# Binary cross-entropy on one core: a small side block in 12-row transfers, and a last store of 128 rows

## The chip, the core and the metric

The kernel runs on one core of one Trainium2 chip. The metric is the device time of one execution in microseconds (us). The time before is 1864.81 us, the median of three runs (1864.67 to 1865.51).

## The reference

```python
def setup_inputs():
    return {
        "pred": np.random.uniform(0.01, 0.99, (8192, 8192)).astype(np.float32),
        "target": np.random.randint(0, 2, (8192, 8192)).astype(np.float32),
    }

def reference(pred, target):
    eps = 1e-7
    pred = np.clip(pred, eps, 1 - eps)
    return -(target * np.log(pred) + (1 - target) * np.log(1 - pred))
```

Two float32 matrices of 256 MiB each are read and one is written. Every target is 0 or 1, so the kernel computes -ln|p + t - 1|: for t = 1 that is -ln p, for t = 0 it is -ln(1 - p).

## The kernel before

The matrices are taken as flat runs of elements and cut into 40 chunks in flat order. A chunk of w columns is a tile of 128 partitions by w columns, and each partition's w elements are one contiguous run in memory. `plan` gives the widths: chunks 0 and 1 have 5120 columns (FIRST), chunks 2 to 36 have 14336 (BIG), chunks 37 and 38, named a and b, have 5632 (LAST), and chunk 39, named c, has 1024 (TAIL).

In on-chip memory pred lies in a ring of three BIG slots, `ring_p`, float32, and is turned into the output in place. Target lies in `ring_t`, one BIG slot of bf16. Both have 1024 columns more, behind the slots, for chunk c alone. Chunks a and b lie side by side in the slot that follows that of chunk 36.

For each chunk there are six kinds of steps:

- `load_t` (line 72): a transfer issued by GpSimd, which casts target from float32 to bf16 on its way.
- `load_p` (line 69): issued by GpSimd, and by SyncE for chunk 0 alone.
- `clip` (line 85): one VectorE pass, max and min.
- `log`: on VectorE p = (t - 1) + p (line 91), then Abs and Ln on ScalarE (lines 94 and 95).
- `back` (line 99): VectorE multiplies by -1.
- `store` (line 76): issued by GpSimd, and by SyncE for the last three chunks. Chunk c has `store_rows` (line 81) instead: three SyncE transfers, of 108, 12 and 8 partitions.

The order is written out by hand, inside `manual_schedule`: each engine takes its instructions in the order of the program, and waits only for the data that they need. A BIG chunk goes through `clip` and `log` in two halves (`(h, 2)`). Then the next chunk's target is loaded (it needs `ring_t` free, so it waits for line 91 on both halves), the two halves get `back`, the chunk is stored, and pred of the chunk after next is loaded into the slot that its predecessor in the ring has left. At the end, in iteration 36, target of a and b, pred of c and target of c are loaded in this order; pred of a and b is loaded one iteration earlier. Behind the loop the halves of a and b and the whole of c are interleaved by hand, and the stores of a, b and c go out on SyncE.

DMA transfers are carried out by 16 DMA engines. The profile lists GpSimd's transfers as the queue "software_dynamic" (q0) and SyncE's as "hardware_dynamic" (q1).

Of the kernel before, what the change touches and what calls it, by code (L numbers as in the profile page):

```python
# [1 line left out]

# [4 lines left out]

EPS = 1e-7

BIG = 14 * 1024  # L10
FIRST = 5 * 1024
LAST = 5632
TAIL = 1024
SLOTS = 3


def plan(total):
    n = (total - 2 * FIRST - 2 * LAST - TAIL) // BIG
    assert n > 4 and total == 2 * FIRST + n * BIG + 2 * LAST + TAIL
    spots = [(FIRST, 0, 0), (FIRST, FIRST, FIRST)]  # L20
    spots += [(BIG, k % SLOTS * BIG, 0) for k in range(1, n + 1)]
    end = (n + 1) % SLOTS * BIG
    spots += [(LAST, end, 0), (LAST, end + LAST, LAST)]
    return spots + [(TAIL, SLOTS * BIG, BIG)]


@with_exitstack
def kernel(
    ctx: ExitStack,
    tc: tile.TileContext,  # L30
    pred: bass.AP,
    target: bass.AP,
    out: bass.AP,
):
    nc = tc.nc
    fp32 = mybir.dt.float32
    bf16 = mybir.dt.bfloat16
    Alu = mybir.AluOpType
    Act = mybir.ActivationFunctionType
    P = nc.NUM_PARTITIONS  # L40

    R, C = pred.shape
    spots = plan(R * C // P)
    n = len(spots)
    widths = [s[0] for s in spots]
    cols = [sum(widths[:k]) for k in range(n)]

    def chunk(ap, k):
        flat = ap.rearrange("r c -> (r c)")
        return flat[cols[k] * P : (cols[k] + widths[k]) * P].rearrange("(p w) -> p w", p=P)  # L50

    pool = ctx.enter_context(tc.tile_pool(name="rings", bufs=1))
    ring_p = pool.tile([P, SLOTS * BIG + TAIL], fp32, name="ring_p", tag="ring_p")
    ring_t = pool.tile([P, BIG + TAIL], bf16, name="ring_t", tag="ring_t")
    warm = pool.tile([1, 8], fp32, name="warm", tag="warm")

    def spot(k, part=(0, 1)):
        w, c, _ = spots[k]
        i, m = part
        return ring_p[:, c + i * w // m : c + (i + 1) * w // m]  # L60

    def spot_t(k, part=(0, 1)):
        w, _, c = spots[k]
        i, m = part
        return ring_t[:, c + i * w // m : c + (i + 1) * w // m]

    def load_p(k):
        queue = nc.sync if k == 0 else nc.gpsimd
        queue.dma_start(out=spot(k), in_=chunk(pred, k))  # L69

    def load_t(k):
        nc.gpsimd.dma_start(out=spot_t(k), in_=chunk(target, k))  # L72

    def store(k):
        queue = nc.sync if k >= n - 3 else nc.gpsimd
        queue.dma_start(out=chunk(out, k), in_=spot(k))  # L76

    def store_rows(k):
        src, dst = spot(k), chunk(out, k)
        for first, last in ((0, 108), (108, 120), (120, 128)):  # L80
            nc.sync.dma_start(out=dst[first:last], in_=src[first:last])

    def clip(k, *part):
        p = spot(k, *part)
        nc.vector.tensor_scalar(  # L85
            out=p, in0=p, scalar1=EPS, scalar2=1 - EPS, op0=Alu.max, op1=Alu.min
        )

    def log(k, *part):
        p = spot(k, *part)  # L90
        nc.vector.scalar_tensor_tensor(  # L91
            out=p, in0=spot_t(k, *part), scalar=1.0, in1=p, op0=Alu.subtract, op1=Alu.add
        )
        nc.scalar.activation(out=p, in_=p, func=Act.Abs)  # L94
        nc.scalar.activation(out=p, in_=p, func=Act.Ln)  # L95

    def back(k, *part):
        p = spot(k, *part)
        nc.vector.tensor_scalar(out=p, in0=p, scalar1=-1.0, scalar2=None, op0=Alu.mult)  # L99

    with tc.manual_schedule():
        nc.vector.memset(warm, 1.0)  # L102
        load_t(0)
        load_p(0)
        load_t(1)
        load_p(1)
        load_p(2)
        nc.scalar.activation(out=warm, in_=warm, func=Act.Ln)  # L108
        for k in (0, 1):
            clip(k)  # L110
            log(k)
        load_t(2)
        back(0)
        store(0)
        back(1)
        store(1)
        load_p(3)
        a, b, c = range(n - 3, n)
        for k in range(2, n - 3):
            for h in (0, 1):  # L120
                clip(k, (h, 2))
                log(k, (h, 2))
            if k < n - 4:
                load_t(k + 1)
            else:
                load_t(a)
                load_t(b)
                load_p(c)
                load_t(c)
                back(k, (0, 2))  # L130
                for j in (a, b):
                    clip(j)
            if k < n - 4:
                back(k, (0, 2))
            back(k, (1, 2))
            store(k)
            if k + 2 < n - 3:
                load_p(k + 2)
            elif k + 2 == n - 3:
                load_p(a)  # L140
                load_p(b)
        log(a, (0, 2))
        log(a, (1, 2))
        clip(c)
        log(b, (0, 2))
        back(a, (0, 2))
        log(b, (1, 2))
        back(a, (1, 2))
        store(a)
        log(c)  # L150
        back(b, (0, 2))
        back(b, (1, 2))
        store(b)
        back(c)
        store_rows(c)


# [1 line left out]
_INS = ['pred', 'target']  # L159
_OUTS = [((8192, 8192), 'float32')]  # L160


# [23 lines left out]
```

## Time and profile before

| | |
|---|---|
| median of three runs | 1864.81 us (1864.67 to 1865.51) |
| the profiled execution's own time | 1864.33 us |
| its span, first to last instruction | 1862.6 us |
| VectorE (DVE) busy | 1121.6 us, 60% |
| ScalarE (ACT) busy | 902.4 us, 48% |
| GpSimd (POOL) busy | 178.5 us, 10% |
| bytes read from and written to HBM | 536.87 and 268.44 MB, 432 GB/s over the span |
| DMA packets | 17302, of which 592 in SyncE's queue |
| a BIG pred load, issue to landing | 44.3 us |
| a BIG target load, issue to landing | 31.3 us |
| a BIG store, issue to landing | 31.1 us |

Times are counted from the start of the span. An engine's busy time doesn't count waiting or the issuing of DMAs by a sequencer (SPq is SyncE's). The DMA row of the slices gives the mean busy share of the 16 DMA engines in tenths, where 9 is 90% or more. The GB/s in it counts what arrives, so a target load counts half of what it reads. The profile's rows carry no number of the DMA engine, but the trace has the start, length and size of each packet and the time of each semaphore update: a transfer over all 128 partitions posts 16 of these, one for each DMA engine's share.

### The profile page before, as it was taken

How to read it: one execution, taken by the hardware profiler on the slowest of the kernel's cores; microseconds unless marked ns; L12 is line 12 of the kernel's file. 1: busy time of each engine (PE TensorE's matmuls, PEld its weight loads, DVE VectorE, ACT ScalarE, POOL GpSimd, SP SyncE). 2: the span in 40 equal slices, each digit the busy share in tenths (PEclk: the TensorE clock that was granted, in tenths of full speed). 3: DMA queues.
4: the chain of work that ended last, by engine and by line, in shares of the span. 5: the costliest groups of instructions: out<-in, count | busy, mean ns of one | idle time of the engine just before them, and what ended most of it. 6: DMA issues, size and time to landing. Idle time of an engine off the chain costs nothing.

```text
span 1862.6 us, 707 instructions
## 1 busy us (share of the span) xinstructions
DVE 1121.6 (60%) x230; ACT 902.4 (48%) x156; POOL 178.5 (10%) x120
## 2 busy tenths in 40 slices
DVE  4666555555666566555555666566655555666565
ACT  4454444455555544444455555544444445555545
POOL 1111101111110011101111110011101111110020
DMA  9999999999999999999999999999999999999999
GB/s 346 347 371 355 356 352 355 356 355 354 359 375 374 375 372 355 355 355 355 355 355 355 357 374 374 374 372 355 355 356 355 357 357 356 357 373 376 375 352 356
DMA packets 17302, 671.15 MB, mean 360 GB/s; under 512 B 1936, under 2 KB 1936, under 8 KB 2320
## 3 DMA queue, kind: packets, MB, share of 16 engines
q0 software_dynamic: 16704, 662.18, 99.1%
q1 hardware_dynamic: 592, 8.91, 1.1%
q14 instruction: 6, 0.05, 0.0%
HBM read 536.87 MB, written 268.44 MB: 432 GB/s over the span
## 4 chain that ended last, share of the span: by engine, by line
DMA 60%; issue 35%; ACT 3%; DVE 2%; POOL 0%; POOLq 0%; DVEq 0%; PEldq 0%
DMA ring_t<-in_target_dram 57%; DMA ring_p<-in_pred_dram 4%; ACT ring_p L95 1%; ACT ring_p L94 1%; DVE ring_p L91 1%; DVE ring_p L99 0%; DVE ring_p L85 0%; POOL out_dram L76 0%; POOL ring_t L72 0%; POOLq L72 0%; POOL ring_p L69 0%; POOLq L76 0%; DVEq L91 0%; PEldq L181 0%
## 5 line engine op out<-in xcount | busy, mean ns | idle before, releaser
L94 ACT ACTIVATE ring_p<-ring_p 128x7168 f32<-128x7168 f32 (+3 forms) x77 | 452.0, 5870 | 942.1 <-DVE ring_p L91 942.1
L91 DVE SCALAR_TENSOR_TENSOR ring_p<-ring_t,ring_p 128x7168 f32<-128x7168 bf16 (+3 forms) x77 | 558.2, 7251 | 372.5 <-DMA ring_t<-in_target_dram 371.3
L99 DVE TENSOR_SCALAR ring_p<-ring_p 128x7168 f32<-128x7168 f32 (+3 forms) x77 | 285.4, 3706 | 329.4 <-ACT ring_p L95 329.4
L95 ACT ACTIVATE ring_p<-ring_p 128x7168 f32<-128x7168 f32 (+3 forms) x77 | 452.5, 5877 | 2.4
L85 DVE TENSOR_SCALAR ring_p<-ring_p 128x7168 f32<-128x7168 f32 (+3 forms) x75 | 284.6, 3794 | 24.0 <-DMA ring_p<-in_pred_dram 24.0
L76 POOL DMA_DIRECT2D out_dram<-ring_p x37 | 128.0, 3459 | 584.4 <-DVE ring_p L99 584.3
L72 POOL DMA_DIRECT2D ring_t<-in_target_dram x40 | 28.9, 722 | 1057.5 <-DVE ring_p L91 1056.7
L69 POOL DMA_DIRECT2D ring_p<-in_pred_dram x39 | 21.7, 558 | 2.5 <-issue 2.5
L108 ACT ACT_TABLE_LOAD x1 | 1.3, 1283 | 0.7 <-PEq L170 0.7
L102 DVE MEMSET warm<- 1x8 f32 x1 | 0.1, 65 | 0.8 <-PEq L170 0.8
L108 ACT ACTIVATE warm<-warm 1x8 f32<-1x8 f32 x1 | 0.2, 208 | 0.0
L170 POOL MEMSET const-float32-0.0<- 128x1 f32 x1 | 0.1, 99 | 0.2 <-issue 0.2
L170 POOL MEMSET const-bfloat16-1.0<- 128x1 bf16 x1 | 0.1, 102 | 0.0
L170 POOL MEMSET const-float32-1.0<- 128x1 f32 x1 | 0.1, 99 | 0.0
L170 POOL MEMSET const-uint8-127<- 128x1 uint8 x1 | 0.1, 99 | 0.0
## 6 DMA issues: line engine op xcount, KB each, us to landing
ring_p<-in_pred_dram POOLq DMA_DIRECT2D x35, 7168.0 KB, 44.3
out_dram<-ring_p POOLq DMA_DIRECT2D x35, 7168.0 KB, 31.1
ring_t<-in_target_dram POOLq DMA_DIRECT2D x35, 3584.0 KB, 31.3
ring_p<-in_pred_dram POOLq DMA_DIRECT2D x2, 2816.0 KB, 37.2
out_dram<-ring_p SPq DMA_DIRECT2D x2, 2816.0 KB, 14.7
out_dram<-ring_p POOLq DMA_DIRECT2D x2, 2560.0 KB, 28.7
ring_t<-in_target_dram POOLq DMA_DIRECT2D x2, 1408.0 KB, 26.5
ring_p<-in_pred_dram SPq DMA_DIRECT2D x1, 2560.0 KB, 13.1
```

The lines of the kernel that those rows point to most:

```text
L69: queue.dma_start(out=spot(k), in_=chunk(pred, k))
L72: nc.gpsimd.dma_start(out=spot_t(k), in_=chunk(target, k))
L76: queue.dma_start(out=chunk(out, k), in_=spot(k))
L85: nc.vector.tensor_scalar(out=p, in0=p, scalar1=EPS, scalar2=1 - EPS, op0=Alu.max, op1=Alu.min)
L91: nc.vector.scalar_tensor_tensor(out=p, in0=spot_t(k, *part), scalar=1.0, in1=p, op0=Alu.subtract, op1=Alu.add)
L94: nc.scalar.activation(out=p, in_=p, func=Act.Abs)
L95: nc.scalar.activation(out=p, in_=p, func=Act.Ln)
L99: nc.vector.tensor_scalar(out=p, in0=p, scalar1=-1.0, scalar2=None, op0=Alu.mult)
L102: nc.vector.memset(warm, 1.0)
L108: nc.scalar.activation(out=warm, in_=warm, func=Act.Ln)
L170: nc = _bacc.Bacc("TRN2", target_bir_lowering=False, num_devices=1)
```

## The change

A block of 24 rows by 896 columns, the last 21504 elements of the matrices, is taken out of chunk c, which becomes 856 columns wide (1024 - 24 x 896 / 128). It has two tiles of its own, `side_p` and `side_t`, both float32 and 128 by 896, of which only 24 partitions carry data: partitions 0, 9, ..., 99 the first 12 rows, partitions 1, 10, ..., 100 the other 12. VectorE fills both tiles with constants at launch (0 and 0.5), since the passes over them run on all 128 partitions.

Side is loaded at launch by four SyncE transfers of 12 rows, right after SyncE's load of chunk 0. It is clipped and goes through `log` in iteration 4, after that chunk's own passes, and through `back` after that chunk's store. It is stored by two SyncE transfers of 12 rows, between the stores of a and b.

Chunk c moves into the slots of a and b, behind b, in both rings. Pred of c is loaded right after pred of a and b, instead of between the target loads of b and c. Its store is one SyncE transfer of 128 partitions, instead of three.

```diff
-TAIL = 1024
+SIDE = 896
+TAIL = 1024 - 24 * SIDE // 128
...
-    return spots + [(TAIL, SLOTS * BIG, BIG)]
+    return spots + [(TAIL, end + 2 * LAST, 2 * LAST)]
...
-    ring_p = pool.tile([P, SLOTS * BIG + TAIL], fp32, name="ring_p", tag="ring_p")
-    ring_t = pool.tile([P, BIG + TAIL], bf16, name="ring_t", tag="ring_t")
+    ring_p = pool.tile([P, SLOTS * BIG], fp32, name="ring_p", tag="ring_p")
+    ring_t = pool.tile([P, BIG], bf16, name="ring_t", tag="ring_t")
+    side_p = pool.tile([P, SIDE], fp32, name="side_p", tag="side_p")
+    side_t = pool.tile([P, SIDE], fp32, name="side_t", tag="side_t")
...
+    def side(ap, j):
+        flat = ap.rearrange("r c -> (r c)")
+        first = R * C - (2 - j) * 12 * SIDE
+        return flat[first : first + 12 * SIDE].rearrange("(p w) -> p w", w=SIDE)
+
+    def side_rows(tile_, j):
+        return tile_[j : j + 100 : 9, :]
...
-    def store_rows(k):
-        src, dst = spot(k), chunk(out, k)
-        for first, last in ((0, 108), (108, 120), (120, 128)):
-            nc.sync.dma_start(out=dst[first:last], in_=src[first:last])
+    def load_side():
+        for j in (0, 1):
+            nc.sync.dma_start(out=side_rows(side_t, j), in_=side(target, j))
+            nc.sync.dma_start(out=side_rows(side_p, j), in_=side(pred, j))
+
+    def store_side():
+        for j in (0, 1):
+            nc.sync.dma_start(out=side(out, j), in_=side_rows(side_p, j))
...
         nc.vector.memset(warm, 1.0)
+        nc.vector.memset(side_t, 0.0)
+        nc.vector.memset(side_p, 0.5)
         load_t(0)
         load_p(0)
+        load_side()
...
             for h in (0, 1):
                 clip(k, (h, 2))
                 log(k, (h, 2))
+            if k == 4:
+                clip_of(side_p)
+                log_of(side_p, side_t)
             if k < n - 4:
                 load_t(k + 1)
             else:
                 load_t(a)
                 load_t(b)
-                load_p(c)
                 load_t(c)
...
             back(k, (1, 2))
             store(k)
+            if k == 4:
+                back_of(side_p)
             if k + 2 < n - 3:
                 load_p(k + 2)
             elif k + 2 == n - 3:
                 load_p(a)
                 load_p(b)
+                load_p(c)
...
         store(a)
+        store_side()
         log(c)
         back(b, (0, 2))
         back(b, (1, 2))
         store(b)
         back(c)
-        store_rows(c)
+        store(c)
```

`clip_of`, `log_of` and `back_of` are the bodies of `clip`, `log` and `back`, taking tiles instead of a chunk's number.

## The prediction

> **What bounds the kernel now.** I read the page's slices and queues first, then a table of stretches of the trace, then the timeline of the end, and last the single packets and semaphore updates that the trace records. The page:
>
> ```profile
> span 1862.6 us, 707 instructions
> ...
> DVE 1121.6 (60%) x230; ACT 902.4 (48%) x156; POOL 178.5 (10%) x120
> ...
> DMA  9999999999999999999999999999999999999999
> ...
> q0 software_dynamic: 16704, 662.18, 99.1%
> q1 hardware_dynamic: 592, 8.91, 1.1%
> ```
>
> No compute engine passes 60%, the DMA engines are full in every slice, and nearly all of their time is GpSimd's queue (q0); SyncE's (q1) has 1.1%. The stretches (length, busy us of DVE, ACT and POOL, clock, share of the 16 DMA engines, GB/s) say it more sharply:
>
> ```profile
> 4.00:8.00 4.00, 0.00 (x0) 0.00 (x0) 0.00 (x0) 1.00 1.00 346
> 8.00:60.00 52.00, 26.00 (x7) 17.88 (x4) 7.25 (x4) 1.00 1.04 321
> 60.00:900.00 840.00, 513.24 (x100) 413.78 (x68) 75.29 (x49) 1.00 1.00 363
> ...
> 1830.00:1845.00 15.00, 12.41 (x7) 14.90 (x7) 0.00 (x0) 1.00 1.00 430
> 1845.00:1855.00 10.00, 2.32 (x2) 2.57 (x3) 0.00 (x0) 1.00 0.99 426
> ...
> 1859.00:1860.00 1.00, 0.00 (x0) 0.00 (x0) 0.00 (x0) 1.00 0.83 332
> 1860.00:1861.00 1.00, 0.00 (x0) 0.00 (x0) 0.00 (x0) 1.00 0.21 84
> ```
>
> From 4 to 1855 us all 16 DMA engines work without a gap, and the last compute ends at 1848.3, some 13 us before the end. So the chain of waits, which runs through compute, isn't what sets the end here. The time is one engine's work: a first packet at 1.76 us, then packets end to end until the slowest engine is through. A change moves the time only if it changes the slowest engine's total or opens a gap.
>
> The engines aren't equally fast. Each transfer over all 128 rows posts 16 completions. In the middle of the run twelve come within 1.6 us (eleven within 0.95), three at 2.5 and one at 3.2 us after the first. The lag was 1.4 us at 15 us, 2.6 at 160, 3.0 at 260 and 3.2 from about 500 us on. The final store is cut into 108, 12 and 8 rows, and q1 has 80 end marks: three whole transfers make 48, so the pieces used 12, 12 and 8 engines. At the end the twelve that lag least finish store(b) by 1859.88, and post the last piece by 1861.67; the other four post store(b) only at 1860.81 to 1861.49. Nine rows of the first piece take 9 x 0.159 = 1.43 us, so an engine that ends (b) at 1860.81 would post them at 1862.2; all were posted by 1861.29. So the four slow engines carry no row of the last store. It is balanced to 0.18 us: 1861.67 for the twelve, 1861.49 for the four.
>
> **The change, part by part.** Sums are against the profiled execution, 1864.33 us (span 1862.6 and 1.7 around it), which is 0.48 below the median of 1864.81; I add the difference found to the median.
>
> *Work of each DMA engine.* Packet times from the trace: 4096 bytes 0.159 us, 22528 bytes 0.836, a straight line between them, so a 3584-byte side row 0.140 and a 3424-byte row (856 columns) 0.134. A target row of 1024 columns took 0.173, of 5632 columns 0.851, so 856 columns take 0.148. A transfer of 128 rows puts 8 rows on each engine; an end mark is 0.009.
> - The four slow engines, before: 8 x 0.173 for the last target chunk, 8 x 0.159 for pred, no store: 2.66 us. After: 8 x 0.148 + 8 x 0.134 + 8 x 0.134 + 0.01 = 3.34. They get **0.68 more**, provided the six side transfers miss them.
> - The slowest of the twelve (it posts one of the 8-row piece's completions), before: 1.384 + 1.272 + 11 x 0.159 + 0.03 = 4.43. After: 3.34 + 6 x (0.140 + 0.009) = 4.23. It gets **0.20 less**.
> So the four end at 1861.49 + 0.68 = 1862.17, the slowest of the twelve at 1861.47. The end moves from 1861.67 to 1862.17: **+0.50 us**. Reading the side target as float32 instead of bf16 doesn't matter at this size: the HBM bytes read are the same, and a 28672-byte bf16 packet took 2.131 us against 2.116 for the float32 one that holds as many columns.
>
> That the side transfers use the same twelve engines is taken from the 12-row piece of before, which posted twelve landings, all among the fast ones. The Trainium skill (DMA: Bandwidth & Descriptors, "Why a DMA increments its semaphore by 16 and not by 1") says that a SyncE transfer runs on the lowest-numbered k engines, k being the largest number up to 16 that divides the row counts, which is 12 here; GpSimd's small transfers move round instead. Were they to use all 16 engines in turn, the four would get three quarters of 6 x 0.149, that is 0.67 us more, and the sum would be +1.17.
>
> Rows of 3424 bytes no longer start at multiples of 4096, which no row of before shows. A gain is excluded, as 0.134 is already on the line of the long rows; for the loss the widest difference between packets of equal HBM bytes is the bound (0.159 against 0.173, 9%): 24 x 0.134 x 9% = 0.3 us. I take 0, because rows of 22528 bytes, which start at multiples of 2048 only, run as fast per byte as those of 20480 (0.836 and 0.761).
>
> *Launch.* SyncE's load_p(0) still goes first. The four side loads wait for two VectorE fills of 128x896. No such fill is shown; between the warm fill (0.065 us) and the clip of 1024 columns scaled (0.694 x 896/1024 = 0.61) I take the latter: about 1.2 us from 0.87 on. Behind the waiting SyncE stands nothing until store(a) at 1839.8. VectorE has until 13.88. What a VectorE pass can cost GpSimd: stores' issues took 3.63 us beside a clip and 0.54 us beside L91. If the fills hold load_t(0) up by up to 1 us, q0's first packet (5.31 us) comes at 6.3; load_p(0) alone feeds each engine with 8 x 0.774 = 6.2 us from 1.8 on, so until 8.0. Cost 0; without that cover, 1 us. The side packets give the twelve 4 x 0.149 = 0.60 us; that is in the sum. Chunk 0's compute comes up to 0.6 later, and load_t(2), issued at 37.0, finds about 10 us queued (26.9 to landing, 17.0 of it own packets).
>
> *Chunk 4.* VectorE gets a clip (0.61), an L91 pass (1.218 x 0.875 = 1.07) and a negation (0.61), ScalarE two passes of 0.92. After L91's second half VectorE is idle for 0.99 us until ScalarE releases back: back's first half comes 0.7 us later, its second half waits 8.38 us for ScalarE as before, so store(4) isn't late. Side's passes stand behind ScalarE's second half. load_t(5) and load_p(6) can be held up 0.6 us beside the short passes; the queue in front of a target load is 31.3 - 8 x 2.131 = 14 us. The next L91 pass has 11 us of idle before it. Cost 0; with no cover, some 1.3 us.
>
> *End.* load_p(c) moves ahead of load_t(a) and load_t(b) on GpSimd's queue, into the slot of a and b, which is freed for them anyway. Before:
>
> ```profile
> 1822.25 6.09 DVE L91 SCALAR_TENSOR_TENSOR ring_p<-ring_t,ring_p 128x2816 f32<-128x2816 bf16 x2
> ...
> 1829.97 0.69 DVE L85 TENSOR_SCALAR ring_p<-ring_p 128x1024 f32<-128x1024 f32 x1 [1.63 <-DMA ring_p<-in_pred_dram]
> ...
> 1839.77 7.82 SPq L76 DMA_DIRECT2D out_dram<-ring_p  x2
> ...
> 1847.64 0.69 DVE L99 TENSOR_SCALAR ring_p<-ring_p 128x1024 f32<-128x1024 f32 x1 [0.41 <-ACT ring_p L95]
> 1848.36 1.41 SPq L81 DMA_DIRECT2D out_dram<-ring_p  x3
> ```
>
> VectorE's wait of 1.63 for pred of c goes. In its place target of a, landed at 1822.05, comes 8 x 0.134 = 1.07 later, so log(a) starts about 1 us later; ScalarE's eight passes follow back to back, so store(b), issued at 1847.3, goes at about 1848.4, and store(a), bound by VectorE, some 0.5 us earlier than 1839.8. Packets of a occupy the fastest engine until 1851.27, and side's two rows follow them; a SyncE issue led to packets 1.0 us later at launch. So b has some 2 us of cover, and c over 7. One issue of 128 rows replaces three (1.41 us). All of it costs 0; were the cover gone, 1 us.
>
> **The rivals.**
> 1. *The launch relief is lost.* The lag stopped growing at 3.2 us, which speaks for a steady state that the engines fall back to; then the 0.60 us that the four gain on the twelve at launch is gone by the end: +1.10, 1865.9. Against it: the growth came in steps at certain times, like fixed delays. Chance 0.15.
> 2. *The four's lag shrinks*, because its growth until 500 us meets engines that stand otherwise to each other; the slowest of the twelve then sets the end at 1861.47: -0.2, 1864.6. The most that it can give is perfect balance: the engines' last packets ended at 1860.3 in the mean and 1861.3 at the latest, and the mean work grows by 0.06, so -0.9, 1863.9. Chance 0.12.
> 3. *Slower: 12 rows at a step of 9 partitions land on one engine.* The strided SBUF side is the one thing that the 12-row piece of before doesn't show. Then one engine gets 72 packets of 0.140, 10.1 us, and if it is one that finishes store(b) first, at 1858.39, it has little over 3 us of room. With its 0.4 less at c's loads and c's store at 1.08, it ends near 1858.4 - 0.4 + 10.1 + 1.1 = 1869.2: +7.5, 1872.3. It decides if a transfer uses one engine; two would give +2.5. The trace speaks against it: 108, 12 and 8 rows each spread by their counts. Chance 0.04.
> 4. *Each small transfer costs a fixed time with the engines empty.* Before has three pieces after store(b), the change six and a whole store, four more transfers. The time from a SyncE issue to its first packet is 1.0 us, so four would give +4.0, 1868.8. Against: packets of the pieces followed each other on their engines with 0.009 us marks between. Chance 0.02. The Trainium skill (DMA: Bandwidth & Descriptors, "Rules for kernel authors") speaks against the change here: under 64 KB one pays mostly overhead. [...]
>
> **How the numbers follow.** The forecast, +0.5, has the remaining 0.66: **1865.3 us**. With the spread of the three runs (-0.14 to +0.70) and 0.3 for the rows its own range is 1865.2 to 1866.3. Rival 1 with the same spread reaches 1866.9, rival 2 half way to perfect balance 1864.1 (between -0.2 and -0.9, less the 0.14); 3, 4 and the rest stay out. A difference of 0.2% (3.7 us) is about what a measurement tells from no change: forecast, 1 and 2 are within: 0.93. Slower: 3, 4, nothing else: 0.06. Faster by 3.7 us needs DMA bytes to go, and none do: 0.01, left for what I overlook.
>
> **What would show it.** Right: DMA share 1.00 from 4 to 1855 us; side transfers of before's rate on twelve engines (12 landings each); the four's lag at mid-run about 0.6 us smaller (2.6); at the end the four last, by some 0.7 us; the wait of 1.63 gone. Rival 1 shows a lag of 3.2 at mid-run. Wrong: fewer than 12 landings of a side transfer, a slice of DMA below 9, or a gap between stores a and b.

## The result, and the profile after

The changed kernel takes 1867.82 us (median of 22 executions, 1866.31 to 1871.13), the kernel before in the same comparison 1864.84 us (22 executions, 1864.26 to 1865.65). The ratio is 1.0017, with a 95% interval of 1.0011 to 1.0023: about 3.0 us slower, where 0.5 was forecast and the range ended at 1866.9. The executions also lie further apart, 4.8 us against 1.4.

The page of the changed kernel, the same rows as before:

```profile
span 1866.0 us, 724 instructions
...
DVE 1125.1 (60%) x235; ACT 903.9 (48%) x158; POOL 179.4 (10%) x120
...
DMA  9999999999999999999999999999999999999998
...
q0 software_dynamic: 16640, 662.05, 98.9%
q1 hardware_dynamic: 720, 9.09, 1.2%
```

Nothing in it tells why: the DMA engines are as full, the engines as idle, 1.2% instead of 1.1% of the time is SyncE's queue. Only the last slice is an 8. The stretches (length, busy us of DVE, ACT and POOL, clock, DMA share, GB/s):

```profile
4.00:8.00 4.00, 0.00 (x0) 0.00 (x0) 0.00 (x0) 1.00 1.00 343
...
60.00:900.00 840.00, 515.32 (x103) 414.26 (x70) 75.80 (x49) 1.00 1.00 363
900.00:1700.00 800.00, 481.26 (x95) 380.92 (x63) 74.22 (x47) 1.00 1.00 360
...
1859.00:1860.00 1.00, 0.00 (x0) 0.00 (x0) 0.00 (x0) 1.00 0.86 354
1860.00:1861.00 1.00, 0.00 (x0) 0.00 (x0) 0.00 (x0) 1.00 0.32 133
1861.00:1862.60 1.60, 0.00 (x0) 0.00 (x0) 0.00 (x0) 1.00 0.15 64
1862.60:1866.00 3.40, 0.00 (x0) 0.00 (x0) 0.00 (x0) 1.00 0.04 15
```

In the stretches shown from 4 to 1700 us the DMA share is 1.00, so no gap was opened. What is new is the tail of the table. At 1860 us most engines are through, as before. But a few go on: 0.15 of the engines from 1861 to 1862.6, and some still after that, where before had next to none:

```profile
1861.00:1862.60 1.60, 0.00 (x0) 0.00 (x0) 0.00 (x0) 1.00 0.01 3
```

The last landing is at 1864.77 (before: 1861.67). So the loss isn't a wait on the compute engines; it is that a few DMA engines are behind the others.

How far behind, the semaphore updates tell: the lag is, for a GpSimd transfer over 128 rows, the time from its first to its last of 16 completions. Below, in us, the lag at some points of the run (also in us):

```
                 21    250   500   940   1100  1500  1750
before          1.36  2.61  3.11  3.15  3.20  3.21  3.20
after           0.59  0.95  2.63  3.71  4.13  4.77  4.72
```

The side loads do what they were reckoned to do at launch: they take the twelve engines 0.6 us back, and at 21 us the slowest is 0.59 behind the first instead of 1.36. But this level doesn't last. The lag grows, passes 3.2 at about 750 us, and goes on until 1500, where that of before had all but stopped by 500.

*Where it grows.* A target packet takes 2.131 us. After 80 us before has 23 that took over 40 ns longer, all ahead of 520 us; after has 77, of which 32 lie behind 600 us, the last at 1579. All 77 are among the last 16 packets of a load of 128, so each is its engine's last one, or for an engine far behind at times the one ahead of it, before it turns to the store that stands next in GpSimd's queue (of before's 23, 22 are among the last 16). The stretches are 0.04 to 0.56 us each. An engine that meets several of them falls back by some us; here nothing brings it forward again.

The trace doesn't number the engines, but a packet starts where the one before it on its engine ends, so that packets can be joined into 16 chains. From 108 to 1732 us the two chains furthest behind in after fell back by 3.99 and 3.56 us, and their stretched packets sum to 4.10 and 3.43. In before, from 107 to 513 us, the four furthest behind fell back by 1.07 to 1.59 us with stretched packets of 1.03 to 1.59. So the stretched packets are what the lag grows by.

### The profile page after: what moved, and what is told of

The parts are those of the page before. It is cut to its first block, busy times and chain, and to the rows that moved or that the text cites. A ratio compares the mean times of both kernels' runs of the same rounds, so it can differ in the third digit from the quotient of the medians.

```text
span 1866.0 us, 724 instructions
## 1 busy us (share of the span) xinstructions
DVE 1125.1 (60%) x235; ACT 903.9 (48%) x158; POOL 179.4 (10%) x120
## 4 chain that ended last, share of the span: by engine, by line
DMA 61%; issue 36%; ACT 1%; DVE 1%; POOL 0%; POOLq 0%; DVEq 0%; PEldq 0%
DMA ring_t<-in_target_dram 60%; DMA ring_p<-in_pred_dram 1%; DVE ring_p L104 1%; ACT ring_p L108 1%; ACT ring_p L107 1%; DVE ring_p L99 0%; POOL ring_t L83 0%; DVE ring_p L111 0%; POOLq L83 0%; POOLq L87 0%; DVEq L104 0%; PEldq L211 0%
```

## The experiments

The lag, the stretched packets behind 600 us (number and sum) and, where there is a 12-row transfer or a 108-row piece near the end, the time between the first and the last of its twelve engines, all from one profiled execution each; the times are medians, the difference is to the kernel before in the same comparison. The range is that of 22 executions for before and after and of 10 or 11 for the others; the last two rows are second traces, of one execution each:

| kernel | time, us | difference | range | lag at 21 us | lag at 1750 us | stretched after 600 us | the twelve apart at the end |
|---|---|---|---|---|---|---|---|
| before | 1864.84 | | 1.4 | 1.36 | 3.20 | 0 | 1.51 |
| after | 1867.82 | +2.98 | 4.8 | 0.59 | 4.72 | 32, 5.68 us | 4.74 |
| e1_launch_only | 1867.72 | +2.52 | 3.0 | 1.16 | 4.70 | 24, 3.72 us | 5.60 |
| e2_no_side | 1865.79 | +0.59 | 1.3 | 1.32 | 3.69 | 1, 0.21 us | |
| e3_side16 | 1866.43 | +1.23 | 1.0 | 1.32 | 3.80 | 6, 0.94 us | |
| e4_side_mid | 1866.14 | +0.94 | 1.0 | 1.52 | 3.13 | 0 | 1.78 |
| e5_launch_x4 | 1869.29 | +4.25 | 2.0 | 1.12 | 4.25 | 33, 5.80 us | |
| e6_launch_half | 1866.27 | +1.23 | 1.4 | 0.98 | 4.55 | 14, 3.64 us | 3.20 |
| e9_start_gpsimd | 1866.13 | +0.93 | 1.6 | 1.71 | 4.02 | 1, 0.08 us | 1.54 |
| e11_before_again | 1865.35 | | | 1.19 | 3.90 | 12, 1.88 us | 2.57 |
| e12_after_again | 1873.77 | | | 0.87 | 8.86 | 67, 19.20 us | 3.38 |

One trace differs from the next of the same kernel (lag 3.20 and 3.90 for before, 4.72 and 8.86 for after), so a lag between 3.2 and 3.9 tells nothing apart.

**e1: the launch loads alone.** `dummy` issues one SyncE load of 12 rows into the third slot of `ring_p`.

```diff
...
+        nc.vector.memset(ring_p[:, 2 * BIG : 2 * BIG + 896], 0.0)
+        nc.vector.memset(ring_p[:, 2 * BIG + 896 : 2 * BIG + 1792], 0.5)
         load_t(0)
         load_p(0)
+        for j in (0, 1):
+            dummy(target, j, 0)
+            dummy(pred, j, 1)
```

> The kernel before, with nothing of the change but four loads of 12 rows at launch (and the two fills); they land in a slot that nobody reads. Theory A (the launch loads set the engines level, and level engines go on losing time in the last packet of each target load): lag of the slowest engine about 0.6 us at 20 us, 4 or more at the end of the run, time 1867 to 1869 us, runs apart by 2 us or more. Theory B (the new places, order and store of chunk c, or the side block's other parts, make the difference): the twelve engines get 0.6 us more, time about 1865.4, runs within 1.5 us, lag at most 3.3.

The ratio is 1.0015 (1.0006 to 1.0023), and the executions are 3.0 us apart. Theory A's time and spread came; B's 1865.4 didn't. The lag ends at 4.70 as expected. At 21 us it was 1.16, not 0.6: fourteen engines were within 0.32, two behind. So four loads of 43 KB that nobody reads cost 2.5 us. Not all of that is lag: in e1's trace the slowest engine is one of the twelve. The last rows land 1.58 us after store(b) (1865.96 against 1864.38), where in before they land 0.18 us after it, as the four that were slowest there have no rows left. That is 1.4 of the 4.3 us by which the last landing of this trace is later. The changed kernel has another tail, so the 2.5 can't simply be taken out of its 3.0.

**e2: everything but side.** The changed kernel with TAIL = 1024 and without the side block, its passes and its transfers.

> The changed kernel without the side block: chunk c has 1024 columns in its new place, pred of c is loaded early, the last store is one of 128 rows. Theory A: lag as in the kernel before (1.4 us at 20 us, 3.2 in the middle); the four engines get 8 x 0.159 us more, so they end at 1862.8, time about +1.1, 1865.9, runs within 1.5 us. Theory B: 1867 or more, and as far apart as the changed kernel's.

1.0003 (0.9994 to 1.0012): no difference that this comparison shows. The interval is wide enough for the summed +1.1 and for 1867 too; but no execution was above 1866.77 and all lie within 1.3 us, which speaks against B. The lag starts as before's and stands still from 500 us on (3.68 to 3.71).

**e3: side on all 16 engines.**

```diff
-SIDE = 896
+SIDE = 672
...
-        first = R * C - (2 - j) * 12 * SIDE
+        first = R * C - (2 - j) * 16 * SIDE
...
-        return tile_[j : j + 100 : 9, :]
+        return tile_[j : j + 121 : 8, :]
```

(TAIL is counted for 32 rows.)

> The changed kernel with side as 32 rows of 672 columns, moved in transfers of 16 rows, so that each goes to all 16 engines and levels nothing. Each engine gets six packets of some 0.11 us. Theory A: lag at 20 us 1.3, in the middle about 3.2; time 1861.5 + 0.7 + 0.7 for the last engine, so +1.2, 1866.0, runs within 1.5 us. Theory B: about 1867.8, with the changed kernel's spread.

1.0006 (0.9997 to 1.0015), +1.23 where +1.2 was summed, executions 1.0 apart. The bytes, the place and the time of the loads are those of the changed kernel; the rows are shorter (672 columns, and so are side's passes), and the loads go to all engines. The lag starts at 1.32. So it isn't small transfers at launch that cost, but that they fall on twelve engines and not on the other four.

**e4: the same twelve, but later.**

```diff
-        nc.vector.memset(side_t, 0.0)
-        nc.vector.memset(side_p, 0.5)
...
-        load_side()
...
-            if k == 4:
+            if k == 20:
+                nc.vector.memset(side_t, 0.0)
+                nc.vector.memset(side_p, 0.5)
+                load_side()
+            if k == 24:
                 clip_of(side_p)
...
-            if k == 4:
+            if k == 24:
                 back_of(side_p)
```

> The changed kernel with side's fills and loads in iteration 20 (about 950 us) and its passes in iteration 24. Theory A: lag 3.2 until then, as before, and about 2.6 after, with perhaps some new growth; time 1865.3 to 1866, runs within 1.5 us. Theory B: about 1867.8, with the changed kernel's spread, since all of it but the time of the loads is the same.

1.0006 (0.9997 to 1.0014), +0.94, and 1866.14 is a little over the 1866 expected at most. The trace shows what my sum had assumed for the launch: the lag is 3.58 at 936 us, the loads take the twelve back, it is 3.09 at 1106 and 3.13 at 1750, and no target packet is stretched after 600 us. So the relief lasts when it comes after the lag has settled (in this one trace; the kernel is no faster than before for it).

**e5 and e6: more and less of it.** e1 with sixteen such loads, and with two.

> The kernel before with four times the launch loads of e1_launch_only (16 of 12 rows, 2.4 us on each of the twelve engines), landing in a slot that nobody reads. Theory A (what harms is that the engines stand level): the other four now lead by some 1.8 us, so nothing is level between the groups; the twelve end 2.4 us later than before, time about 1867.6, no growth of the lag after 600 us. Theory C (each launch load on twelve engines costs in proportion, 2.5 us for the four of e1): +10, about 1875.

> The kernel before with half of the launch loads of e1_launch_only (two of 12 rows, 0.3 us on each of the twelve). Theory A: half levelled, so the four start 0.3 us behind; lag at the end between before's 3.2 and the changed kernel's 4.8, time between 1865.5 and 1867.5. Theory C: +1.2, about 1866.4, with before's spread.

Half gives +1.23, ratio 1.0006 (0.9998 to 1.0015), and can't be told from before, nor from e3, by its time; the twelve are 3.20 apart at its end, between the 1.51 of before and e1's 5.60. Four times gives +4.25, ratio 1.0023 (1.0014 to 1.0032). C's 1875 is far off: the cost isn't in proportion. But A's 1867.6 without growth is off too: the lag was 2.65 at 245 us and 4.25 at 1751, with 33 stretched packets behind 600 us. Here the other four lead (at 46 us three are 1.4 to 1.7 us ahead of the first of the twelve, one 0.65), nothing is level between the groups, and the lag still grows. So "level" isn't the right word for what harms. What e1, e5, e6 and the change share, and e2, e3 and e4 don't, is a delay of the twelve alone at launch. For e6 only the trace says so.

**e7 and e8: a pred load between target load and store.**

```diff
-            back(k, (1, 2))
-            store(k)
             if k + 2 < n - 3:
                 load_p(k + 2)
...
                 load_p(a)
                 load_p(b)
+            back(k, (1, 2))
+            store(k)
```

The new order has a wait that the old one hadn't, for the store of the previous chunk to land and free the slot; the engines stay full all the same (DMA share 1.00 and 1.01 in the two stretches below; the wait's row has us in total, times and the longest):

```profile
POOL ring_p L69 <- DMA out_dram<-ring_p: 471.9, 33, 15.4
...
60.00:900.00 840.00, 513.39 (x100) 409.97 (x67) 102.03 (x49) 1.00 1.00 363
900.00:1700.00 800.00, 478.50 (x94) 380.50 (x63) 101.74 (x47) 1.00 1.01 361
```

> The kernel before with load_p(k + 2) issued ahead of store(k), so that on GpSimd's queue a pred load and not a store follows each target load. If the lost time of the last target packet comes from the other engines' writing to HBM beside it, the last target packets are no longer stretched and the lag at 500 us stays near its start of 1.4 us; the stretching could then show in the last pred packets. If it belongs to the target load itself (its cast), it stays as it is, with lag 3.2. Time within 1 us of before in either case.

> e7_pred_first with the launch loads of e1_launch_only. If the store behind the target load is what stretches the packet: lag at the end about 0.6 to 1.5 us and time at most 0.6 over e7_pred_first. If not: as e1_launch_only, about 2.5 us over before, runs 2 us or more apart.

The stretched target packets go from 23 to 1. In their place 80 packets of 57344 bytes are stretched (before: 2), and 78 of them end while a pred load lands, or at most 0.4 us ahead of its first completion: it is now the pred load that stands ahead of the store, and its last packets are the long ones. So it isn't the cast or the target load; it is the last load packet ahead of a store, whichever it is. Neither the time nor the lag stayed where they were expected: 1869.93, ratio 1.0025 (1.0015 to 1.0035), lag 5.74 at 500 us and 8.47 at 1748. e8 took 1872.55, 1.0040 (1.0026 to 1.0054), 2.6 over e7, so the launch loads cost about the same time in either order. But not by more lag: e8's is 8.57. Its slowest engine is one of the twelve and gets the last rows (1.8 us after store(b), against 0.7 in e7). Why pred packets lose more than target packets in that place is open.

**e9: another start.** The kernel before with chunk 0's pred load on GpSimd's queue too.

> The kernel before with chunk 0's pred load on GpSimd's queue, so that no SyncE transfer sets when each engine starts. All engines then start with q0's first packets at about 5.3 us instead of 1.8: +3.5 us in any case, 1868.5. Theory D (engines that start behind slip on at each change from loads to stores; who they are is decided at launch): another start gives other lags; if the start is level within 0.6 us, laggards also among the twelve engines of the 12-row pieces (those spread by over 2 us at the end), time 1869 to 1871. Rival E (four fixed engines are slow whatever the start): the twelve stay within 1.6 us of each other at the end, time 1868.5.

The premise was wrong: with no SyncE load ahead of it q0's first packet came at 2.6 us, not at 5.3; the time is +0.93, 1.0005 (0.9996 to 1.0014). The start wasn't level (1.71), and the same picture as in the kernel before came: four engines behind, the twelve 1.54 apart at the end. That speaks for E in one point: which engines start behind doesn't hang on SyncE's load. D wasn't put to the test.

**e10: stores and loads mixed.** The kernel before with all stores on SyncE's queue.

> The kernel before with every store on SyncE's queue, so that stores run packet by packet beside loads, with no common change from loads to stores. If it is that change which stretches the last load packets, few packets are stretched singly, the lag stays near its 1.4 us, and the time is within 1 us of before or below it. If reading beside writing is what costs, all packets are longer and the time rises by more than 5 us.

The time is 2136.97, ratio 1.1452 (1.1433 to 1.1471). Its page:

```profile
span 2136.0 us, 744 instructions
...
DMA  9998999989898989999898989898998989898997
...
q0 software_dynamic: 11376, 400.04, 62.6%
q1 hardware_dynamic: 5920, 271.06, 30.5%
```

The first expectation fails and the second holds in the time, though not all packets are longer: after 80 us 1484 of 4480 pred packets, 589 of 4480 target packets and 1223 of 4480 store packets took over 40 ns longer (1184, 353 and 370 us in sum), together 1907 us over 16 engines, 119 us of each. (For the rest of the 272 us the slices show 8: there are gaps now, which I didn't follow further.) So both kinds get longer where engines load and store side by side, loads more than stores. In the kernel before that happens for some us at each change from loads to stores, to the engines that come last.

**e11 and e12: second traces.**

> The kernel before once more, for a second trace. Theory D and rival E: lag about 3 us from 500 us on, the twelve engines of the first 12-row piece within 2 us of each other at the end.

> The changed kernel once more, for a second trace. Theory D: start level within about 0.6 us at 20 us, growth past 600 us, and the twelve engines of the side stores apart by over 3 us. Rival E: those twelve within 2 us.

The kernel before took 1865.35: lag 3.41 at 500 us, 3.90 at 1750, 12 stretched packets behind 600 us (1.88 us in sum), the twelve 2.57 apart at the end. That is a little more than either theory expected. The changed kernel took 1873.77, beyond its 22 earlier executions: 0.87 at 21 us, then 3.03, 4.32, 6.47 and 8.86 at 250, 500, 940 and 1750, with 67 stretched packets behind 600 us, 19.20 us in sum. Here 78 packets of 57344 bytes took over 40 ns longer too, 19.38 us in sum, all but three behind 600 us (4 in the first trace), and 53 of them ended while a store was landing, or at most 0.4 us ahead of its first completion, nearly all from 1490 us on. So with a lag of 7.7 us (at 1496) and more, packets get longer at the change back from stores to loads as well. The twelve are 3.38 apart. But this time the slowest engine of all, 2.8 us behind the next, isn't among them: store(a) landed from 1856.77 to 1862.96, while the side rows behind it had all landed by 1860.57. So the part of theory D by which the lag is handed to the twelve doesn't always hold. It can fall on either group.

## Why the prediction was wrong

**What failed.** The step was "So the four end at 1861.49 + 0.68 = 1862.17, the slowest of the twelve at 1861.47". It takes the places of the engines at the end of before and adds the change's work to each. That holds only if the lag is a given of each engine. It isn't, and "The engines aren't equally fast" was a wrong reading: of before's 3.20 us at the end, 1.36 were there at 21 us and the rest came from stretched last load packets, nearly all in the first 500 us, and a delay of the twelve at launch changed who was stretched, how often and until when. The first completions of the transfers late in the run came 0.8 us later than before, about the 0.6 of the side loads (1748.9 against 1748.1); the last 2.3 us later (1753.65 against 1751.34). These 2.3 are the term that was missing.

The slowest engine is also another one than the step has. Three of the four that are furthest behind post side rows (their shares of store(a) land at 1853.66, 1854.34 and 1856.73, their side rows 0.19 later), so they are of the twelve; the fourth (1856.19) isn't. The slowest of the twelve, forecast at 1861.47, ended at 1864.77; the slowest of the four, forecast at 1862.17, at 1863.95. The slowest has the tail's 0.68 and its two side rows' 0.30 to do. With the 2.31, and less the 0.18 by which the four ended ahead in before, that is the 3.1 by which the last landing moved (1864.77 against 1861.67).

**Rival 1** came nearest: the launch relief is lost. But it let the four lose their 0.60 again and stop at 3.2. The growth doesn't stop there (4.72 and 8.86 in two traces), and it isn't the four that end last in the first of them. My remark that the growth "came in steps at certain times, like fixed delays" was an error of reading: the steps are stretched packets at the change from loads to stores, once in 50.75 us, and which engines they hit changed with the loads at launch. Each was in the trace of before, as a packet that took longer than 2.131. Rival 2, a shrinking lag, didn't come.

**What held.**
- The twelve engines: each side load and each side store posted twelve landings, close together at launch, so rival 3 was out. The rule of the Trainium skill (DMA: Bandwidth & Descriptors, "Why a DMA increments its semaphore by 16 and not by 1") gives k = 12 here, and the trace agrees with 12 landings and one early update.
- The tail's sum: with the launch part taken out, e2 (+0.59, summed +1.1), e3 (+1.23, summed +1.2) and e4 (+0.94, summed +0.5) are within 0.5 us of it, though none of the three can be told from no change by its interval.
- The covers. The fills and issues at launch open no gap: q0's first packet is at 5.34 (before 5.31). The rows of the launch in the timeline of after:

```profile
1.03 0.81 DVE L124 MEMSET side_t<- 128x896 f32 x1 [0.16 <-issue]
...
1.86 0.89 SPq L91 DMA_DIRECT2D side_t<-in_target_dram  x1
1.97 0.81 DVE L125 MEMSET side_p<- 128x896 f32 x1
...
4.34 0.72 SPq L92 DMA_DIRECT2D side_p<-in_pred_dram  x1
...
13.61 2.83 DVE L99 TENSOR_SCALAR ring_p<-ring_p 128x5120 f32<-128x5120 f32 x1 [10.84 <-DMA ring_p<-in_pred_dram]
```

A fill took 0.81 us, more than the 0.61 that I took; VectorE had until 13.6 all the same. Rival 4's fixed price of small transfers has no place: the four were issued 0.75 to 0.94 us apart, and the engines stayed full.
- The wait for pred of c is gone, as the timeline of the end shows:

```profile
1825.45 6.09 DVE L104 SCALAR_TENSOR_TENSOR ring_p<-ring_t,ring_p 128x2816 f32<-128x2816 bf16 x2 [0.74 <-DMA ring_t<-in_target_dram]
...
1831.46 0.60 DVE L99 TENSOR_SCALAR ring_p<-ring_p 128x856 f32<-128x856 f32 x1
...
1841.32 0.34 SPq L87 DMA_DIRECT2D out_dram<-ring_p  x1
1841.71 7.02 SPq L96 DMA_DIRECT2D out_dram<-side_p  x2
...
1850.46 1.53 SPq L87 DMA_DIRECT2D out_dram<-ring_p  x2
```

The clip of c stands without a bracket, and log(a) has got a wait for its target (0.74). But log(a) starts 3.2 us later than before, not 1, and store(a) is issued 1.5 later instead of 0.5 earlier: a load lands when its slowest engine does, and that is 1.5 us further behind the first, which is itself 0.7 later. The covers took it: no gap shows between stores a and b.

**What stays open.** That a delay of the twelve at launch sets the growth off is shown by the traces of the change, e1, e5 and e6, which have it, and of e2, e3 and e4, which don't. Why it does, isn't: "level engines" fell with e5. What is seen at 500 us in most of the kernels that stop growing early is that a group of four stands together, three at 2.4 to 2.9 us behind and the slowest at 3.1 to 4.0, about one packet of 2.1 us or a little more; in the changed kernel it was two engines, in e12 one. But e6 has such a four, too (2.76 to 3.75), and still went on to 4.55. No run here tells what the reason is.

## What to carry to other kernels

Where all DMA engines are full from start to end, as here, the time is that of the slowest one, and its lag is part of the profile: the spread of a transfer's completions over the run, and the packets that took longer than their kind, tell where it comes from before one adds work to it. A relief of some engines is better tried at a point where the lag has settled (e4) than ahead of what makes it (e1). A tail that is cut to fit the engines that lag should be checked against a second trace: which engines these are can change. Loads and stores in one queue and in long stretches did best here; each change from one to the other cost the engines that come last up to some tenths of a us, and mixing them cost 14.5% (e10, gaps included).

## What the runs showed of the hardware

- The last load packet of an engine ahead of a store, 2.131 us alone, took up to 0.69 us more in the kernel before, 0.56 in the changed kernel, and 0.83 in its second trace, at the change to stores; with loads and stores mixed throughout (e10), pred packets of 2.116 us took 0.27 us more in the mean and the kernel 14.5%.
- A shift of twelve engines by 0.6 us at launch was worth 2.5 us at the end of the run (e1), and made executions of the same program differ by 3.0 us (e1) and 4.8 us (the changed kernel) instead of 1.4; e5 and e6 differed by 2.0 and 1.4.
- A GpSimd queue's first packet came at 2.6 us when no SyncE load was issued ahead of it (e9), and at 5.3 us beside a SyncE load that was issued 0.5 us ahead of it.
